# A decoder step's sample tokens: retention state on VectorE with transposed states, and each stream's second head pair bound to its own first

## The chip, the cores and the metric

The kernel runs on one core of a Trainium2 chip. The metric is device time in microseconds of one execution, the median of several runs. The profile shows one further execution, instruction by instruction. TensorE (PE) multiplies matrices into PSUM, VectorE (DVE) and ScalarE (ACT) do element work, SyncE (SP) issues nearly all DMAs from one in-order queue, and GpSimd (POOL) does almost nothing here.

## The reference

Two layers of a decoder trunk, for a prompt of 512 tokens and for 8 sample tokens (one new token of each of 8 sequences, each with its own state). Every layer is half an FFN, a token mixer, half an FFN, each with a layer norm. The mixer of layer 0 has four retention heads beside an RG-LRU; that of layer 1 is a pooling mixer. The part that matters is the retention step:

```python
q = rotary(q, pos) * (RET_DK ** -0.5); k = rotary(k, pos)
...
def step(s, qkv):          # one chunk; for a sample token the chunk has length 1
    scores = einsum('bhid,bhjd->bhij', qc, kc) * decay
    o = einsum('bhij,bhjv->bhiv', scores, vc) + einsum('bhid,bhdv->bhiv', qc * q_dec, s)
    s = s * c_dec + einsum('bhjd,bhjv->bhdv', kc * k_dec, vc)
    return s, o
...
mu = mean(o, -1); var = mean(square(o - mu), -1)
o = (o - mu) * rsqrt(var + LN_EPS) * gn_g
ret_out = silu(g) * o
```

For a sample token and a head with decay gamma this is: new state S' = gamma S + k v^T (128x128 for each of the 8 sequences), output o = S'^T q. The new states are outputs of the kernel too.

## The kernel before, in words

The 520 tokens are two streams that share the weights: stream A (s = 0) holds prompt tokens 0 to 255, stream B (s = 1) prompt tokens 256 to 511 and the 8 sample tokens, so matmuls of A have 256 columns and those of B 264. Features lie on partitions. A weight block arrives by DMA as raw fp32 (`load`, L422) in one of 36 SBUF slots, ACT rounds it to `hi` and DVE computes `lo` = raw - hi (`prep`, L434), and a *unit* (`emit`, L540) is 24 matmuls (hi x hi, hi x lo, lo x hi for eight 128-blocks) into one of five PSUM buffers `ps`, which ACT or DVE then evacuates. Everything else uses three more PSUM buffers `pm`.

The mixer of layer 0 has for each stream 4 units `ux`, then per head 4 units (q, k, v, g), with 4 units `ug` between heads 1 and 2 (`MIX_ORDER`), then 8 output units (`mk_mixout`). Around the units run generator tasks: `lru_task`, `ret_task` (retention of one head and stream) and `ret_finish` (group norm and gate of a pair of heads, 0 and 1 or 2 and 3). A small planner (`run`, L508) steps units and tasks in a virtual time and so sets the order in which instructions are emitted, in which slots are claimed (`get`, `slot`, `drop`) and weights prefetched (`wcap`, `dma_ahead`). Each task carries a priority offset (`D_RET = -200`, ...). The Tile layer then places the instructions on the engines by readiness and priority, so that the order on an engine can differ from that of emission; each engine runs its own list in order.

The sample tokens of a head are handled by `sample_ret` (L1187), called at the end of `ret_task` of stream B (L1139):

- the old states are loaded as S0[k, b, v], k on partitions, 512 bytes a run (L1193);
- k and v of the 8 tokens are transposed on PE (L1196, L1197); ACT copies k, DVE writes v times an 8x8 mask into an 8x1024 block VB (L1201);
- two matmuls with 8 rows and 512 columns form k v^T for four sequences each (L1209), and DVE adds gamma S0 (L1212, 128x512 twice);
- the new state is stored (L1215), and for each token one matmul of one column with S0 as the stationary operand gives o (L1220); ACT copies it, a matmul with the matrix of 1/128 gives its mean (L1228), which DVE subtracts (L1230).

Only then does `ret_task` set `retdone` and go on into `ret_finish`. In the unit list, the q unit of heads 2 and 3 waits for the flag `retdone1` of head h - 2 (L809), and `ret_finish` sets it for **both** streams at its end in stream B (L1183 to L1185): 

```python
dep=[("retdone1", h - 2)] if j == 0 and h >= 2 else []      # L809
...
            if s == 1:                                       # L1183
                self.flags[("retdone1", h, 0)] = 0.0
                self.flags[("retdone1", h, 1)] = 0.0
```

Of the kernel before, what the change touches and what calls it, by code (L numbers as in the profile page):

```python
# [58 lines left out]
D_LRU = 0  # L59
D_RET = -200  # L60
D_LN = 0
D_POOL = 0
D_PREP = 100
D_PREPP = 500
# [31 lines left out]
class Build:  # L96
    def __init__(self, ctx, tc, ins, outs):
        self.tc, self.nc = tc, tc.nc
        self.ins, self.outs = ins, outs
        self.t_pe = self.t_dve = self.t_act = self.t_pool = 0.0  # L100
        self.cpool = ctx.enter_context(tc.tile_pool(name="cp", bufs=1))
        self.spool = ctx.enter_context(tc.tile_pool(name="sp", bufs=NSLOT))
        self.tpool = ctx.enter_context(tc.tile_pool(name="tp", bufs=2))
        self.pp = ctx.enter_context(tc.tile_pool(name="pp", bufs=5, space=bass.MemoryType.PSUM))
        self.pm = ctx.enter_context(tc.tile_pool(name="pm", bufs=3, space=bass.MemoryType.PSUM))
        self.free = NSLOT
        self.wused = 0
        self.pmfree = 3
        self.tasks = []
        self.uid = 0  # L110
        self.flags = {}
        self.ntask = 0
        self.pin = False
# [107 lines left out]
    def alloc(self):  # L221
# [17 lines left out]
        self.HTAIL = [self.const(f"htail{s}", [P, 4]) for s in range(2)]  # L239
        self.US = self.const("us", [P, 4, NS])  # L240
        self.HS = self.const("hs", [P, 4, NS])
        self.SMP = self.const("smp", [P, 4, HEADS, NS])
        self.sp4 = self.const("sp4", [P, 4])
        self.pbs = self.const("pbs", [P, NCH])
        self.pss = self.const("pss", [P, NCH])
# [774 lines left out]
    def mk_qkvg(self, h, j):  # L1020
        def evac(s, ps, T):
# [7 lines left out]
            if j < 2:  # L1029
                sw = self.tmp("e")  # L1030
                rt = self.tmp("e")
                self.act(Tm(T.t), sw[0:64, :n], ps[64:128, :n])
                self.act(T, sw[64:128, :n], ps[0:64, :n])
                o = OFF[s]
                self.tt(Tm(T.t), rt[:, :n], ps[:, :n], self.cos[:, o:o + n], ALU.mult)
                self.tt(T, sw[:, :n], sw[:, :n], self.sin[:, o:o + n], ALU.mult)
                self.tt(T, qk[:, j, :], rt[:, :HALF], sw[:, :HALF], ALU.add)
                if s == 1:
                    self.tt(T, self.SMP[:, j, h, :], rt[:, HALF:n], sw[:, HALF:n], ALU.add)
                    if j == 0:  # L1040
                        self.ts(T, self.SMP[:, j, h, :], self.SMP[:, j, h, :], QSCALE, ALU.mult)
            else:
                f = AF.Copy if j == 2 else AF.Silu
                self.act(T, qk[:, j, :], ps[:, :HALF], f)
                if s == 1:
                    self.act(T, self.SMP[:, j, h, :], ps[:, HALF:n], f)
            if j == 2:
                self.spawn(self.ret_task(h, s, T), d=D_RET)
            if j == 3:
                self.flags[("sg", h, s)] = T.t  # L1050
        return evac
# [6 lines left out]
    def ret_task(self, h, s, T):  # L1058
# [11 lines left out]
        if h % 2 == 0:  # L1070
            self.RP[s] = self.slot([P, 4, NN[1]])
        B = self.RP[s]
        scs = self.slot([P, 4, HALF])
        ob = B[:, h % 2, :n]
        kt = B[:, 2 + h % 2, :HALF].rearrange("p (c k) -> p c k", c=2)
# [55 lines left out]
        if s == 0:  # L1131
            self.SPART[h] = so
        else:
            pa = self.SPART.pop(h)
            self.tt(Ts, so[:], so[:], pa[:], ALU.add)
            self.ts(Ts, so[:, :P], so[:, :P], so[:, P:P + 1], ALU.add)
            nc.sync.dma_start(self.outs["retp"][h], so[:, :P])
            yield ("v", None)
            yield from self.sample_ret(h, ob, scs, T)  # L1139
        self.drop(1)  # L1140
        self.flags[("retdone", h, s)] = T.t
        if h % 2:
            yield from self.ret_finish(h // 2, s, T)

    def ret_finish(self, pr, s, T):
        n = NN[s]
        B = self.RP[s]
        yield from self.get(1)
        Q = self.slot([P, 4, NN[1]])
# [30 lines left out]
            self.drop(1 + pr)  # L1180
        for h in (2 * pr, 2 * pr + 1):
            self.flags[("ret", h, s)] = T.t
            if s == 1:  # L1183
                self.flags[("retdone1", h, 0)] = 0.0
                self.flags[("retdone1", h, 1)] = 0.0  # L1185

    def sample_ret(self, h, ob, scs, T):  # L1187
        nc = self.nc
        yield from self.get(1)
        S0 = self.slot([P, NS, P])  # L1190
        VB = scs.rearrange("p a b -> p (a b)").rearrange("p (b v) -> p b v", b=NS)
        T0 = Tm(self.t_pe + 5.0)
        nc.sync.dma_start(S0[:], self.ins["sret"][0, :, h, :, :].rearrange("b k v -> k b v"))  # L1193
        yield from self.pmget(1)
        pk = self.pmt()
        self.tr(pk[:NS, :P], self.SMP[:, 1, h, :])  # L1196
        self.tr(pk[:NS, P:2 * P], self.SMP[:, 2, h, :])  # L1197
        Tk = Tm(self.t_pe + .1)
        ks = self.tpool.tile([NS, P], F32, tag="ks", name=self.nm("ks"), bufs=2)
        self.act(Tk, ks[:], pk[:NS, :P])  # L1200
        self.tt(Tk, VB[:NS, :, :], pk[:NS, P:2 * P].rearrange("p (a v) -> p a v", a=1).to_broadcast([NS, NS, P]),  # L1201
                self.s("mask8")[:NS, :].rearrange("p (b a) -> p b a", a=1).to_broadcast([NS, NS, P]), ALU.mult)
        self.pmfree += 1
        Tk.t = max(Tk.t, T0.t)
        yield ("pe", Tk)
        for hf in range(2):
            yield from self.pmget(1)
            po = self.pmt()
            self.mm(po[:], ks[:], VB[:NS, 4 * hf:4 * hf + 4, :].rearrange("p b v -> p (b v)"), True, True)  # L1209
            T.t = max(T.t, self.t_pe + 0.1)  # L1210
            sv = S0[:, 4 * hf:4 * hf + 4, :].rearrange("p b v -> p (b v)")
            self.stt(T, sv, sv, GAMMA[h], po[:], ALU.mult, ALU.add)  # L1212
            self.pmfree += 1
            yield ("v", None)
        nc.sync.dma_start(self.outs["rets"][:, h, :, :].rearrange("b k v -> k b v"), S0[:])  # L1215
        yield from self.pmget(1)
        yield ("pe", T)
        pq = self.pmt()
        for b in range(NS):
            self.mm(pq[:, b:b + 1], S0[:, b, :], self.SMP[:, 0, h, b:b + 1], True, True)  # L1220
        T.t = self.t_pe + .1
        self.drop(1)
        self.act(T, ob[:, HALF:NN[1]], pq[:, :NS])
        self.pmfree += 1
        yield from self.pmget(1)
        yield ("pe", T)
        pq = self.pmt()
        self.mm(pq[:, :NS], self.s("ones"), ob[:, HALF:NN[1]], True, True)  # L1228
        T.t = self.t_pe + .1
        self.tt(T, ob[:, HALF:NN[1]], ob[:, HALF:NN[1]], pq[:, :NS], ALU.subtract)  # L1230
        self.pmfree += 1


    def pool_task(self, s, T):
# [56 lines left out]

_OUT_SHAPES = dict(
    y=(P, NCH, NTOK), retp=(HEADS, P, P), hp=(P, 4), convp=(P, 4, 3), poolp=(P, NCH, PB),
    rets=(NS, HEADS, P, P), hs=(P, 4, NS), convs=(P, 4, 3, NS), pools=(P, NCH, NS, PB))


def _tables():
# [26 lines left out]
def _pack(i):  # L1324
# [36 lines left out]
    def put(n, a):  # L1361
# [23 lines left out]
    lruw = np.concatenate([i["lru_wa"][0], i["lru_wi"][0]], 0).transpose(1, 0, 2)  # L1385
    spool = i["state_pool"][0].reshape(NS, PB, NCH, P).transpose(3, 2, 0, 1)
    return dict(xa=xT[:, :, :HALF], xb=xT[:, :, HALF:], w8=np.stack(w8), w7=np.stack(w7), small=sm, lruw=lruw,
                rot=np.stack([cos, sin], 1), dec=dec, sret=i["state_ret"], spool=spool)


# [30 lines left out]
```

## Time and profile before

| | |
|---|---|
| median of 3 runs | 1837.92 us (1837.45 to 1840.04) |
| the profiled execution | 1838.75 us |
| its span, first to last instruction | 1836.8 us |
| PE / ACT / DVE / POOL busy | 98% / 38% / 49% / 0% of the span |
| mean granted TensorE clock | 0.99 of full speed |
| mixer of layer 0, roughly | 395 to 650 us of the span |

Read it from the top: PE is busy almost throughout, so a microsecond of PE work is a microsecond of time wherever PE does not wait. "Idle before" and a name in brackets say what an instruction of that engine waited for. The granted clock is 1.00 when the throttle lets TensorE run at its upper level (2.4 GHz) and 0.50 at the lower (1.2 GHz).

### The profile page before, as it was taken

The numbers are of one execution on the slowest core, as the hardware profiler recorded it, in microseconds if no ns is written. First come the engines' busy times: TensorE is split into PE (matmuls) and PEld (weight loads), VectorE is DVE, ScalarE is ACT, GpSimd is POOL, SyncE is SP. The second block draws the span as 40 slices with busy tenths as digits, with TensorE's granted clock in tenths as the row PEclk, the third lists the DMA queues.
The fourth block names the chain that finished last, engine by engine and source line by source line (L and its number), as shares of the span: only waits on it lengthen the run. The fifth ranks groups of instructions, "written<-read, shape, count | busy, mean of one in ns | idle before, by whom it ended". The sixth has DMA issues, their size and how long they took to land.

```text
span 1836.8 us, 33833 instructions
## 1 busy us (share of the span) xinstructions
PE 1798.1 (98%) x14727; PEld 1773.8 (97%) x14727; DVE 909.1 (49%) x1629; ACT 691.4 (38%) x1210; POOL 2.1 (0%) x10
## 2 busy tenths in 40 slices
PE   8999999999899999999999999999999899999997
PEld 8999999999889999999999999999999799999997
DVE  5443343497665884333335833333347843333336
ACT  5322222266654573222223732222225742222223
POOL 0000000000000000000000000000000000000000
PEclk9999999999989999999999999999999999999998
DMA  7323232223042422322322323223259822323311
GB/s 262 93 84 96 87 102 84 73 88 104 1 162 96 140 77 88 90 93 91 102 83 91 106 82 101 91 85 104 74 81 98 71 89 96 93 87 98 97 31 47
DMA packets 77380, 170.74 MB, mean 93 GB/s; under 512 B 24368, under 2 KB 37168, under 8 KB 77232
## 3 DMA queue, kind: packets, MB, share of 16 engines
q1 hardware_dynamic: 77232, 168.58, 32.5%
q8 instruction: 115, 1.88, 0.4%
q14 instruction: 33, 0.27, 0.0%
HBM read 163.44 MB, written 5.12 MB: 92 GB/s over the span
## 4 chain that ended last, share of the span: by engine, by line
PE 86%; DVE 7%; ACT 5%; issue 1%; DMA 0%; SPq 0%; ACTq 0%; DVEq 0%
PE ps L207 83%; PE pm L207 3%; ACT sl L185 3%; DVE sl L190 2%; DVE sl L203 2%; DVE x L190 1%; ACT L692 1%; ACT L185 1%; ACT xh L185 1%; DVE xl L190 0%; DMA x<-in_xa 0%; DVE x L203 0%; ACT x L185 0%; ACT e L185 0%; DVE e L190 0%
## 5 line engine op out<-in xcount | busy, mean ns | idle before, releaser
L207 PE MATMUL ps<-xh,sl 128*128 128x264 f32 (+1 forms) x6400 | 1172.3, 283 | 12.6 <-ACT xh L185 7.0
L207 PEld LDWEIGHTS ps<-xh,sl 128*128 128x128 f32 x6400 | 997.5, 189 | 16.4 <-ACT xh L185 8.1
L207 PE MATMUL ps<-xl,sl 128*128 128x264 f32 (+1 forms) x3200 | 902.9, 283 | 4.1 <-DVE xl L190 3.8
L207 PEld LDWEIGHTS ps<-xl,sl 128*128 128x128 f32 x3200 | 606.6, 190 | 6.5 <-DVE xl L190 5.9
L207 PE MATMUL ps<-sl,sl 128*128 128x264 f32 (+1 forms) x4672 | 586.7, 284 | 4.3 <-DVE sl L203 4.0
L207 PEld LDWEIGHTS ps<-sl,sl 128*128 128x128 f32 x4672 | 569.1, 189 | 8.9 <-DVE sl L203 5.3
L185 ACT ACTIVATE sl<-sl 128x1024 fp32r<-128x1024 f32 (+8 forms) x371 | 348.9, 950 | 461.2 <-PE ps L207 417.1
L190 DVE TENSOR_TENSOR sl<-sl,sl 128x1024 fp32r<-128x1024 f32 (+3 forms) x320 | 373.7, 1174 | 246.3 <-ACT sl L185 226.2
L190 DVE TENSOR_TENSOR e<-sil,ps 128x256 f32<-128x256 f32 (+1 forms) x176 | 74.7, 424 | 300.5 <-PE ps L207 298.5
L203 DVE SCALAR_TENSOR_TENSOR x<-ps,x 128x256 f32<-128x256 f32 (+1 forms) x208 | 88.5, 426 | 240.5 <-PE ps L207 240.4
L185 ACT ACTIVATE sl<-e 128x264 fp32r<-128x264 f32 (+1 forms) x184 | 76.5, 416 | 278.8 <-DVE e L190 277.8
L185 ACT ACTIVATE sil<-ps 128x264 f32<-128x264 f32 (+1 forms) x176 | 67.0, 382 | 188.4 <-PE ps L207 187.4
L190 DVE TENSOR_TENSOR sl<-e,sl 128x264 fp32r<-128x264 f32 (+1 forms) x184 | 78.5, 427 | 61.2 <-ACT sl L185 61.1
L190 DVE TENSOR_TENSOR x<-x,sl 128x512 f32<-128x512 f32 (+2 forms) x136 | 87.1, 677 | 2.8 <-ACT sl L185 1.8
L185 ACT ACTIVATE e<-x 128x256 f32<-128x256 f32 (+1 forms) x87 | 35.2, 416 | 54.2 <-DVE x L203 54.1
L185 ACT ACTIVATE xh<-x,small 128x256 fp32r<-128x256 f32 (+1 forms) x64 | 35.0, 596 | 9.1 <-DVE x L190 9.1
L185 ACT ACTIVATE sl<-pm 128x256 f32<-128x256 f32 (+2 forms) x44 | 15.0, 362 | 49.0 <-PE pm L207 49.0
L190 DVE TENSOR_TENSOR xl<-x,xh 128x512 fp32r<-128x512 f32 (+1 forms) x40 | 27.6, 695 | 6.3 <-ACT xh L185 5.8
L190 DVE TENSOR_TENSOR sl<-sl,e 128x256 f32<-128x256 f32 (+1 forms) x63 | 26.8, 425 | 1.4 <-ACT e L185 0.2
L185 ACT ACTIVATE x<-x,small 128x256 f32<-128x256 f32 (+1 forms) x44 | 25.7, 596 | 4.5 <-DVE x L190 4.3
L185 ACT ACTIVATE e<-ps 64x256 f32<-64x256 f32 (+3 forms) x40 | 15.3, 382 | 24.0 <-PE ps L207 18.4
L203 DVE SCALAR_TENSOR_TENSOR sl<-sl,sl 128x1024 f32<-128x1024 f32 (+3 forms) x14 | 15.0, 1084 | 18.1 <-ACT sl L185 18.0
(115 smaller groups left out, 480.9 us busy)
## 6 DMA issues: line engine op xcount, KB each, us to landing
sl<-in_w SPq DMA_DIRECT2D x241, 512.0 KB, 3.7
sl<-in_w SPq DMA_DIRECT2D x64, 448.0 KB, 3.3
sl<-in_sret SPq DMA_DIRECT2D x4, 512.0 KB, 5.7
out_rets<-sl SPq DMA_DIRECT2D x4, 512.0 KB, 3.6
x<-in_xb SPq DMA_DIRECT2D x2, 528.0 KB, 9.7
out_y<-x SPq DMA_DIRECT2D x4, 264.0 KB, 2.3
x<-in_xa SPq DMA_DIRECT2D x4, 256.0 KB, 6.7
sl<-in_dec SPq DMA_DIRECT2D x2, 512.0 KB, 4.5
```

The lines of the kernel that those rows point to most:

```text
L185: r = self.nc.scalar.activation(out, in_, func, scale=scale, **kw)
L190: r = self.nc.vector.tensor_tensor(out=out, in0=a, in1=b, op=op)
L203: self.nc.vector.scalar_tensor_tensor(out=out, in0=a, scalar=s, in1=b, op0=op0, op1=op1)
L207: self.nc.tensor.matmul(out, lhsT, rhs, start=start, stop=stop)
L692: self.nc.scalar.preload_act_table_set(LNEXP)
```

## The change

The states of the sample tokens are handed over and back by the host as [head][v][b][k] in place of [b][head][k][v], so the tile S0 has v on partitions and, along a partition, 8 tokens by 128 k, in one run of 4 KB.

As soon as k of a head (stream B) is rotated, its 8 q rows and 8 k rows are written transposed to a DRAM tile `KQ` (16 rows of 128, source 128 partitions of 16 elements). A new task `sample_task`, spawned at the v unit of stream B, takes two slots, reads the 8 k rows back broadcast to all 128 partitions (512 KB) and the states (512 KB), multiplies k by v (128x1024, v broadcast along k), adds gamma S0 (128x1024), stores the state, reads the q rows broadcast into the same tile, multiplies by the state and sums over k (128x1024 to 128x8). The mean over v is taken by the matmul with 1/128 as before, and the subtraction writes into the pair's output tile. The two transposes, the two 512-column matmuls and the eight one-column matmuls of each head, the mask product and the two ACT copies are gone.

`ret_finish` becomes a task of its own; for stream B it waits for the two heads' `sdone` flags. `retdone1` is set for the stream that has finished, so heads 2 and 3 of a stream follow that stream's own first pair.

```diff
-        self.SMP = self.const("smp", [P, 4, HEADS, NS])
+        self.SMPH = self.const("smp", [P, HEADS, 4, NS])
+        self.SMP = self.SMPH.rearrange("p h j b -> p j h b")
...
                     if j == 0:
                         self.ts(T, self.SMP[:, j, h, :], self.SMP[:, j, h, :], QSCALE, ALU.mult)
+                    else:
+                        self.KQ[h] = self.dpool.tile([2 * NS, P], F32, tag="kq", name=self.nm("kq"))
+                        self.nc.sync.dma_start(self.KQ[h][:].rearrange("a k -> k a"),
+                                               self.SMPH[:, h, 0:2, :].rearrange("p j b -> p (j b)"))
...
             if j == 2:
                 self.spawn(self.ret_task(h, s, T), d=D_RET)
+                if s == 1:
+                    self.spawn(self.sample_task(h, Tm(T.t)), d=D_SMP)
...
-            yield from self.sample_ret(h, ob, scs, T)
         self.drop(1)
         self.flags[("retdone", h, s)] = T.t
         if h % 2:
-            yield from self.ret_finish(h // 2, s, T)
+            self.spawn(self.ret_finish(h // 2, s, T), d=D_FIN if h == 1 else D_RET)
 
     def ret_finish(self, pr, s, T):
         n = NN[s]
+        while s == 1 and any(("sdone", 2 * pr + e) not in self.flags for e in range(2)):
+            yield ("w", None)
...
-            if s == 1:
-                self.flags[("retdone1", h, 0)] = 0.0
-                self.flags[("retdone1", h, 1)] = 0.0
+            self.flags[("retdone1", h, s)] = 0.0
...
+    def kqb(self, h, j):
+        t = self.KQ[h][j * NS:(j + 1) * NS, :]
+        return t.rearrange("(o b) k -> o b k", o=1).to_broadcast([P, NS, P])
+
+    def sample_task(self, h, T):
+        v = self.SMP[:, 2, h, :].rearrange("p (b a) -> p b a", a=1).to_broadcast([P, NS, P])
+        yield from self.get(2)
+        S0, KB = self.slot([P, NS, P]), self.slot([P, NS, P])
+        self.nc.sync.dma_start(KB[:], self.kqb(h, 1))
+        self.nc.sync.dma_start(S0[:], self.ins["sret"][h])
+        T.t = max(T.t, self.t_pe + SMP_DMA)
+        yield ("v", None)
+        self.tt(T, KB[:], KB[:], v, ALU.mult)
+        yield ("v", None)
+        self.stt(T, S0[:], S0[:], GAMMA[h], KB[:], ALU.mult, ALU.add)
+        self.nc.sync.dma_start(self.outs["rets"][h], S0[:])
+        self.nc.sync.dma_start(KB[:], self.kqb(h, 0))
+        T.t += SMP_DMA
+        yield ("v", None)
+        self.tt(T, KB[:], KB[:], S0[:], ALU.mult)
+        o = self.tpool.tile([P, NS], F32, tag="so8", name=self.nm("so8"), bufs=2)
+        yield ("v", None)
+        self.nc.vector.tensor_reduce(out=o[:], in_=KB[:], axis=AX.X, op=ALU.add)
+        self._adv("t_dve", 1.1, T)
+        self.drop(2)
+        while ("rb", h) not in self.flags:
+            yield ("w", None)
         yield from self.pmget(1)
         yield ("pe", T)
         pq = self.pmt()
-        for b in range(NS):
-            self.mm(pq[:, b:b + 1], S0[:, b, :], self.SMP[:, 0, h, b:b + 1], True, True)
+        self.mm(pq[:, :NS], self.s("ones"), o[:], True, True)
         T.t = self.t_pe + .1
-        self.drop(1)
-        self.act(T, ob[:, HALF:NN[1]], pq[:, :NS])
+        self.tt(T, self.RP[1][:, h % 2, HALF:NN[1]], o[:], pq[:, :NS], ALU.subtract)
...
-                rot=np.stack([cos, sin], 1), dec=dec, sret=i["state_ret"], spool=spool)
+                rot=np.stack([cos, sin], 1), dec=dec, sret=i["state_ret"][0].transpose(1, 3, 0, 2), spool=spool)
```

New constants: `D_SMP = 100`, `D_FIN = 0`, `SMP_DMA = 4.0`. The DRAM pool for `KQ` has two buffers.

## Rows read from the trace of the kernel before

**Rows 1.** The page, part 1: busy us (share of the span) and instructions of each engine.

```profile
PE 1798.1 (98%) x14727; PEld 1773.8 (97%) x14727; DVE 909.1 (49%) x1629; ACT 691.4 (38%) x1210; POOL 2.1 (0%) x10
```

**Rows 2.** Stretches: length, busy us (instructions) per engine, granted clock, DMA share, GB/s.

```profile
482.70:489.50 6.80, 5.34 (x25) 5.34 (x26) 6.55 (x8) 2.25 (x5) 0.00 (x0) 0.50 0.00 0
533.90:540.70 6.80, 6.80 (x29) 6.39 (x29) 1.45 (x4) 3.11 (x7) 0.00 (x0) 0.50 0.98 337
609.00:615.80 6.80, 6.80 (x33) 6.80 (x33) 2.47 (x7) 1.13 (x3) 0.00 (x0) 0.50 0.86 296
440.00:640.00 200.00, 190.13 (x1388) 178.82 (x1388) 141.43 (x315) 104.06 (x208) 0.21 (x1) 0.94 0.31 102
```

**Rows 3.** Timeline of PE around head 0's sample work: start, us, instruction, count.

```profile
502.57 0.38 PE L212 MATMUL pm<-small,smp 128*8 128x128 f32 x2
502.70 0.37 PE L207 MATMUL ps<-xh,sl 128*128 128x264 f32 x1
...
511.39 1.98 PE L207 MATMUL pm<-sl,ks 8*128 8x512 f32 x4
513.30 0.39 PE L207 MATMUL ps<-xh,sl 128*128 128x256 f32 x1
...
514.24 0.95 PE L207 MATMUL pm<-smp,sl 128*128 128x1 f32 x8
515.05 0.37 PE L207 MATMUL ps<-xl,sl 128*128 128x256 f32 x1
```

**Rows 4.** Timeline of PE, head 1's one-column matmuls.

```profile
531.61 1.05 PE L207 MATMUL pm<-smp,sl 128*128 128x1 f32 x8
...
533.44 1.28 PE L207 MATMUL pm<-smp,sl 128*128 128x1 f32 x8
```

**Rows 5.** DVE groups by shape: line, operation, out<-in, count | busy us, mean ns | idle before.

```profile
L203 DVE SCALAR_TENSOR_TENSOR sl<-sl,sl 128x1024 f32<-128x1024 f32 x5 | 6.0, 1225 | 6.8 <-ACT sl L185 6.8
L203 DVE SCALAR_TENSOR_TENSOR sl<-sl,pm 128x512 f32<-128x512 f32 x8 | 5.5, 687 | 2.3 <-PE pm L207 2.3
L190 DVE TENSOR_TENSOR sl<-pm,small 8x1024 f32<-8x1024 f32 x4 | 4.8, 1210 | 0.0
...
L190 DVE TENSOR_TENSOR sl<-sl,sl 128x1024 f32<-128x1024 f32 x3 | 3.7, 1220 | 2.8 <-ACT sl L185 2.8
...
L1271 DVE TENSOR_REDUCE ss<-sl 128x16 f32<-128x240 f32 x1 | 0.4, 394 | 0.0
```

**Rows 6.** DMA issues: queue, operation, count, KB each, median us from issue to landing.

```profile
sl<-in_w SPq DMA_DIRECT2D x241, 512.0 KB, 3.7
sl<-in_sret SPq DMA_DIRECT2D x4, 512.0 KB, 5.7
...
out_retp<-so SPq DMA_DIRECT2D x4, 64.0 KB, 1.5
...
out_pools<-xsm SPq DMA_DIRECT2D x1, 32.0 KB, 21.3
```

**Rows 7.** Waits of SP's queue: line waited for, us in total, times, longest.

```profile
SPq L1137 <- DVE sl L190: 53.2, 1, 53.2
```

**Rows 8.** Timeline of PE: three waits in brackets, second pair's start, stream B's first finish.

```profile
481.74 0.39 PE L207 MATMUL ps<-xh,sl 128*128 128x256 f32 x1 [3.36 <-ACT sl L185]
484.16 0.79 PE L207 MATMUL ps<-xh,sl 128*128 128x256 f32 x2 [1.92 <-DVE sl L190]
...
508.73 0.28 PE L207 MATMUL ps<-xl,sl 128*128 128x256 f32 x1
...
537.55 1.96 PE L207 MATMUL pm<-sl,small 128*128 128x264 f32 x4
...
625.67 0.51 PE L207 MATMUL ps<-sl,sl 128*128 128x264 f32 x2 [0.22 <-ACT sl L185]
```

**Rows 9.** Timeline of DVE: head 3's rotated sample k, and its sample output less the mean.

```profile
584.05 0.16 DVE L190 TENSOR_TENSOR smp<-e,e 128x8 f32<-128x8 f32 x1
...
613.54 0.16 DVE L190 TENSOR_TENSOR sl<-sl,pm 128x8 f32<-128x8 f32 x1 [3.84 <-PE pm L207]
```

More of the change, by code (lines that the diff above doesn't have):

```diff
@@ L61 @@
 D_LN = 0
+D_SMP = 100
+D_FIN = 0
+SMP_DMA = 4.0
 D_POOL = 0
@@ L103, in __init__ @@
         self.tpool = ctx.enter_context(tc.tile_pool(name="tp", bufs=2))
+        self.dpool = ctx.enter_context(tc.tile_pool(name="dp", bufs=2, space=bass.MemoryType.DRAM))
+        self.KQ = {}
         self.pp = ctx.enter_context(tc.tile_pool(name="pp", bufs=5, space=bass.MemoryType.PSUM))
@@ L1072, in ret_task @@
         B = self.RP[s]
+        self.flags[("rb", h) if s else ("ra", h)] = 0.0
         scs = self.slot([P, 4, HALF])
@@ L1182, in ret_finish @@
             self.flags[("ret", h, s)] = T.t
-            if s == 1:
-                self.flags[("retdone1", h, 0)] = 0.0
-                self.flags[("retdone1", h, 1)] = 0.0
[L1187 to L1215, printed above, removed]
@@ L1218, in sample_ret @@
         pq = self.pmt()
-        for b in range(NS):
-            self.mm(pq[:, b:b + 1], S0[:, b, :], self.SMP[:, 0, h, b:b + 1], True, True)
+        self.mm(pq[:, :NS], self.s("ones"), o[:], True, True)
         T.t = self.t_pe + .1
-        self.drop(1)
-        self.act(T, ob[:, HALF:NN[1]], pq[:, :NS])
+        self.tt(T, self.RP[1][:, h % 2, HALF:NN[1]], o[:], pq[:, :NS], ALU.subtract)
         self.pmfree += 1
[L1225 to L1231, printed above, removed]
+        self.flags[("sdone", h)] = T.t
     def pool_task(self, s, T):
@@ L1293 @@
     y=(P, NCH, NTOK), retp=(HEADS, P, P), hp=(P, 4), convp=(P, 4, 3), poolp=(P, NCH, PB),
-    rets=(NS, HEADS, P, P), hs=(P, 4, NS), convs=(P, 4, 3, NS), pools=(P, NCH, NS, PB))
+    rets=(HEADS, P, NS, P), hs=(P, 4, NS), convs=(P, 4, 3, NS), pools=(P, NCH, NS, PB))
 def _tables():
@@ L1414 @@
         np.ascontiguousarray(o["poolp"].transpose(2, 1, 0)).reshape(1, 1, PB, DM),
-        o["rets"].reshape(1, NS, HEADS, P, P),
+        np.ascontiguousarray(o["rets"].transpose(2, 0, 3, 1)).reshape(1, NS, HEADS, P, P),
         np.ascontiguousarray(o["hs"].transpose(2, 1, 0)).reshape(1, NS, 512),
```

## The prediction, made before the change was run

> **What bounds the kernel now.** I read the page's busy shares first. PE is busy 1798.1 of 1836.8 us [rows 1], so PE work that disappears is time that disappears, as long as nothing else becomes late in its place. Then I cut the mixer of layer 0 into stretches. In 440 to 640 us, where everything that the change touches lies, PE is busy 190.1 of 200 us at a mean clock of 0.94, DVE 141.4 and ACT 104.1 [rows 2]. So the stretch has two kinds of loss beside PE's own work: some 10 us of idle PE, and time at the lower clock. Three of the half-clock stretches are 6.8 us long each [rows 2]. The timeline of PE tells what came ahead of each. Ahead of the first, PE idled 3.36 and 1.92 us waiting for the two halves of a weight block, from ACT and from DVE [rows 8]. Ahead of the second stand the sample matmuls of head 1: the first eight one-column records cover 531.61 to 532.66 and the second eight begin at 533.44, just where the clock falls [rows 2, 4]. The third, 609.0 to 615.8, begins in the same work of head 3. That a run of such thin matmuls is what lets the clock fall is an inference: heads 0 and 2 have the same matmuls, more thinly mixed with units, and no such stretch.
>
> **What the change removes from PE.** Head 0 runs at full clock and gives the prices. I take the distance from the start of a piece to the start of the next unit matmul, since PE overlaps instructions. The transposes of k and v take 0.13 us (502.57 to 502.70), the two 512-column matmuls 1.91 (511.39 to 513.30), one half of the one-column matmuls 0.81 (514.24 to 515.05), and so both 1.62 [rows 3]. That is 3.66 us a head, **14.6 us** for four. All of it lies among unit matmuls on a busy PE, so it counts in full. The mean matmul with 1/128 stays.
>
> **What it gives back of the clock.** If PE has only unit matmuls around heads 1 and 3, the two stretches of 6.8 us go, and each had done half of what it could: 3.4 us each, **6.8 us** together [rows 2]. The bounds are 0 (the clock falls anyway) and 6.8; I take 6.8, because the thin matmuls stand right ahead of both.
>
> **What it adds on DVE and takes from DVE and ACT.** Per head two products of 128x1024 at 1.22, one fused multiply-add at 1.225, and one sum over 1024 elements. The nearest row for the sum has 240 elements and 394 ns, by which 1024 would take 1.7 us; as low a price as a plain product, 1.22, bounds it below. I take 1.4, so 5.1 us a head. Gone are two of 0.687 and one of 1.21: 2.6 us [rows 5]. Net 2.5 us a head, 10 us in all, on an engine with 58 us free in this stretch [rows 2]. I cost it at nothing; what hides it is PE's backlog in five PSUM buffers. If DVE were the late engine throughout, it would cost those 10 us. ACT loses two small copies a head, which is worth nothing off the path.
>
> **What it adds in DMA and on SP's queue.** Per head: a write of 8 KB in 2048 runs of 4 bytes, two broadcast reads of 512 KB, the state read and the state write, the last two now in runs of 4 KB. Five issues replace two. The trace has one write with 4-byte runs, 8192 of them, that landed in 21.3 us [rows 6]. A quarter of it gives 5.3 us, and if the count did not matter it would be 21.3; a write of 64 KB in long runs, 1.5 us, is the floor [rows 6]. I take 5.3, as the runs are of the same kind. A broadcast read is in no row. Its bounds are the weight block's 3.7 and the old state read's 5.7 for the same bytes [rows 6], and I take 4.7; 128 reads of the same 4 KB could also be slower than either, and that stays in the range. SP is in order: the k read waits there for the write to land, the state write for DVE's multiply-add, the q read for that too, and the weight loads stand behind them. What that costs is bounded by what SP already bears: a store of head 0's prompt state held the queue for 53.2 us [rows 7], and the waits that PE shows in those 53 us name ACT and DVE halves and no DMA. Waits of 5 to 10 us should cost nothing, so I take 0; if the prefetch ran dry, a hole like that at 481 us would follow (below).
>
> **The new order of the streams.** The flag of the second pair holds back emission, not visibly PE: A's second pair starts at 508.73, 29 us ahead of B's first finish at 537.55 that sets the flag, with unit matmuls on PE up to it [rows 8]. So the edit has no wait of its own to remove. It can still move the hole at 478 to 490 us: if A's q unit of head 2 has its weight halves ready there, PE gains 3.36 + 1.92 = 5.3 idle and, of the half-clock stretch with 5.34 us of work in it, 2.7 more, 8.0 together [rows 2, 8]. If A's lead holds slots and weights longer, one more such hole opens, and it costs 8.0. Two extra slots per head in flight push in the same direction. I take 0, with both ends for the range.
>
> **The end of the mixer.** B's first output unit starts at 625.67 after a wait of only 0.22 [rows 8]: there PE's own work and B's chain (sample output at 613.54, group norm, gate) come out even, so I check both. PE gets there 14.6 + 6.8 = 21.4 us earlier, at about 604.0. Head 3's k is ready at 584.05 [rows 9], and this moves up by three heads' matmuls and one clock stretch, 14.4 us. From k to the sample output I count write 5.3, read 4.7, product and multiply-add 2.4, read 4.7, product and sum 2.6: 19.7 us, to 603.8 in place of 613.54 [rows 9], 9.7 earlier. B's chain is then ready at 625.67 - 14.4 - 9.7 = 601.6, with 2.4 us to spare. With slower reads (5.7 each) and a write of 8 it is 2.3 late, and retention of the prompt tokens may then be last. I take **2 us back**, with 0 and 5 as ends.
>
> **Sum.** 14.6 + 6.8 - 2 = 19.4 us. The profiled execution took 1838.75, 0.83 above the median of the runs shown, 1837.92. So 1837.92 - 19.4 = **1818.5**. Not counted is the slower start of the first unit matmul behind each removed piece, which could add a microsecond. The case itself spans 1811 to 1828.
>
> **Rivals.**
> First, *DVE is held by loads* (slower). The multiplies by k and by q wait for a read from DRAM, eight times. DVE is in order, so a multiply placed too early holds the evacuations of PSUM behind it (rotary products, FFN products, `lo` halves), and PE stops once its five buffers are full. It decides against the change from 19.4 / 8 = 2.4 us of lost PE per wait. If a multiply is placed right behind its issue, DVE waits the whole 3.7 to 5.7; with 4 us lost each, 32 us are lost and the time is about 1850. For it: DVE is the busiest engine after PE here. Against: no DVE row of this stretch waits for a DMA, the old state read included, and some of each wait is covered by PSUM. Chance 0.20, of which 0.03 for mild waits that end near no change.
>
> Second, *the transposing write is the late one*. From a landing of 5.3 + 2.4 = 7.7 us on, B's output units wait for it. At 21.3 the sample output comes 16 us later than counted, B's chain is ready at 617.6, PE idles 13.6 and then runs 3.4 at the lower clock: 1837.92 - 21.4 + 17.0 = 1833.5, within a hair of no change. Chance 0.07.
> The Trainium skill speaks against the change at this place: its page "DMA: Bandwidth & Descriptors", section "Rules for kernel authors", says that a transpose should not be made by a plain DMA with a rearranged access pattern and gives a factor of 19. Applied to the 1.5 us write this is an estimate of 28.5 us and a time of about 1841. By that rule the trace half agrees: 32 KB in 4-byte runs took 21.3 us where 64 KB took 1.5 [rows 6], but the run count here is a quarter.
>
> Third, *the hole at 478 us is filled* by A's second pair: 1818.5 - 8.0 = 1810.5. For it: PE has nothing to do there but wait for weights. Against: it is ACT and DVE that are late there, and they are no earlier. Chance 0.14.
>
> Fourth, *the clock falls anyway*, at a new place or the same: only the matmuls' 14.6 less 2 stay, 1825.3. Chance 0.13. The forecast has 0.46.
>
> **How the numbers follow.** What a measurement of this kernel can tell from no change is about 0.2%, 3.7 us. Faster: 0.46 + 0.14 + 0.13 = 0.73. Within: 0.07 + 0.03 = 0.10. Slower: the rest of the first rival, 0.17. The range runs from 1806 (the filled hole with the uncounted microseconds) to 1840 (the late write and mild DVE waits) and leaves out the bulk of the first rival.
>
> **What would show it.** In the new profile the one-column and 8-row matmuls are absent, and PE has 3.7 us less per head. The stretches around heads 1 and 3 stay at 1.00. No DVE instruction names a DMA as releaser, and PE's waits name no multiply of the sample task. The write lands in about 5 us, the broadcast reads in 4 to 6. B's first output unit starts near 604 with a wait under 5. The forecast is wrong if PE's idle time in the mixer grows by more than 15 us, whatever ends it.

## The result, and the profile after

The changed kernel takes 1861.07 us (median of four runs, 1857.56 to 1864.56) against 1838.2: ratio 1.0126, 95% interval 1.0114 to 1.0139. It is 22.9 us slower where 19.4 us faster was forecast, and above the top of the forecast range, 1840. The profiled execution took 1863.19 us, 24.4 above the one of before (1838.75).

The page's first part for the changed kernel answers [rows 1]: PE is busy 8.1 us less, and the span is 24.3 us longer, so PE waits.

```profile
span 1861.1 us, 33673 instructions
PE 1790.0 (96%) x14639; PEld 1768.3 (95%) x14639; DVE 918.0 (49%) x1633; ACT 690.2 (37%) x1202; POOL 2.1 (0%) x10
```

The mixer of layer 0 up to the same unit (the first of the FFN behind it, 647.8 before, 668.3 after) shows where. Columns as in [rows 2]. Before:

```profile
396.00:648.00 252.00, 241.84 (x1807) 229.47 (x1806) 182.61 (x393) 144.50 (x283) 0.98 (x4) 0.95 0.29 95
```

After, and below it the stretch that answers the last of [rows 2]:

```profile
396.00:668.30 272.30, 231.03 (x1705) 221.53 (x1705) 192.01 (x400) 143.88 (x276) 0.99 (x4) 0.91 0.39 103
440.00:640.00 200.00, 159.02 (x1137) 150.67 (x1136) 131.43 (x285) 92.02 (x180) 0.21 (x1) 0.89 0.45 115
```

The mixer is 20.3 us longer. PE works 10.8 us less in it, although more of the work is at the lower clock (mean 0.91 for 0.95), and idles 41.3 us for 10.2: 31.1 more. The remaining 4 of the 24.3 us lie behind the mixer; I found no cause for them, and executions of this kernel spread over 7 us.

PE's timeline in the mixer of the changed kernel, the waits above 3 us (in brackets the idle time and what ended it):

```profile
458.66 0.39 PE L212 MATMUL ps<-xh,sl 128*128 128x256 f32 x1 [3.80 <-ACT sl L190]
...
488.63 0.58 PE L212 MATMUL ps<-xh,sl 128*128 128x256 f32 x1 [4.62 <-ACT sl L190]
...
568.34 0.58 PE L212 MATMUL ps<-xh,sl 128*128 128x256 f32 x1 [5.38 <-ACT sl L190]
...
607.74 1.22 PE L212 MATMUL pm<-sl,so 128*128 128x256 f32 x2 [9.57 <-DVE sl L195]
...
621.36 0.57 PE L212 MATMUL pm<-so,small 128*128 128x8 f32 x2 [3.76 <-DVE so L1221]
...
639.00 8.86 PE L212 MATMUL ps<-sl,sl 128*128 128x256 f32 x53 [3.81 <-DVE x L208]
```

Before, only the hole at 478 to 490 us was of this size [rows 8]. Two kinds are new. At 458.66 and 568.34 a unit waits for ACT's half of a weight block. From 607.74 on, PE waits for stages of the retention, and at 639.00 for DVE to evacuate an output unit (`x` <- `ps`). The chain of waits says what is behind each (start, us, what):

```profile
444.03 13.50 DMA sl<-in_w
...
553.93 13.28 DMA sl<-in_w
...
589.62 12.26 DMA kq<-smp
601.94 4.17 DMA sl<-kq
```

A weight block that landed in 3.7 us [rows 6] takes over 13 here, twice, and late in the mixer the transposing write takes 12.26 and the broadcast read behind it 4.2. The DMA view gives the landings (count, size, median us):

```profile
sl<-kq SPq DMA_DIRECT2D x8, 512.0 KB, 5.5
...
kq<-smp SPq DMA_DIRECT2D x4, 8.0 KB, 12.2
```

SP's timeline shows why the weights are late: they are issued right behind the write, in the same queue.

```profile
443.56 0.38 SPq L1050 DMA_DIRECT2D kq<-smp  x1
444.03 1.31 SPq L432 DMA_DIRECT2D sl<-in_w  x2
455.56 0.33 SPq L1207 DMA_DIRECT2D sl<-kq  x1
```

ACT's and DVE's timelines show the two engines waiting for these transfers: first ACT for the weights issued at 444.03, then DVE's multiply by the k rows of head 3.

```profile
457.56 1.06 ACT L190 ACTIVATE sl<-sl 128x1024 fp32r<-128x1024 f32 x1 [7.31 <-DMA sl<-in_w]
```

```profile
606.13 1.23 DVE L195 TENSOR_TENSOR sl<-sl,smp 128x1024 f32<-128x1024 f32 x1 [10.15 <-DMA sl<-kq]
```

DVE works its list in order, so this multiply holds up everything behind it. PE's wait of 9.57 us ends at 607.74, 1.6 us after the multiply has started.

### The profile page after: what moved, and what is told of

It reads as the page before. It is cut to its first block, busy times and chain, and to the rows that moved or that the text cites. A ratio compares the mean times of both kernels' runs of the same rounds, so it can differ in the third digit from the quotient of the medians.

```text
span 1861.1 us, 33673 instructions
## 1 busy us (share of the span) xinstructions
PE 1790.0 (96%) x14639; PEld 1768.3 (95%) x14639; DVE 918.0 (49%) x1633; ACT 690.2 (37%) x1202; POOL 2.1 (0%) x10
## 4 chain that ended last, share of the span: by engine, by line
PE 83%; DVE 7%; ACT 6%; DMA 3%; issue 1%; SPq 0%; ACTq 0%; DVEq 0%
PE ps L212 81%; ACT sl L190 3%; DVE sl L195 2%; PE pm L212 2%; DVE sl L208 2%; DMA sl<-in_w 1%; DVE x L195 1%; ACT L698 1%; ACT L190 1%; DMA kq<-smp 1%; ACT xh L190 1%; DMA sl<-kq 1%; DVE xl L195 0%; ACT x L190 0%; DMA x<-in_xa 0%
## 5 line engine op out<-in xcount | busy, mean ns | idle before, releaser
L212 PE MATMUL ps<-xh,sl 128*128 128x264 f32 (+1 forms) x6400 | 1169.0, 283 | 23.3 <-ACT sl L190 13.8
L212 PEld LDWEIGHTS ps<-xh,sl 128*128 128x128 f32 x6400 | 996.3, 189 | 27.1 <-ACT sl L190 14.6
L195 DVE TENSOR_TENSOR sl<-sl,sl 128x1024 fp32r<-128x1024 f32 (+4 forms) x324 | 378.7, 1174 | 258.6 <-ACT sl L190 236.7
L190 ACT ACTIVATE e<-x 128x264 f32<-128x264 f32 (+1 forms) x87 | 34.9, 416 | 56.7 <-DVE x L208 56.5
L190 ACT ACTIVATE sl<-pm 128x256 f32<-128x256 f32 (+1 forms) x40 | 14.4, 382 | 56.6 <-PE pm L212 56.6
L208 DVE SCALAR_TENSOR_TENSOR sl<-sl,sl 128x1024 f32<-128x1024 f32 (+3 forms) x18 | 19.9, 1113 | 21.3 <-ACT sl L190 21.2
```

Of the source, the lines that this page charges most:

```text
L190: r = self.nc.scalar.activation(out, in_, func, scale=scale, **kw)
L195: r = self.nc.vector.tensor_tensor(out=out, in0=a, in1=b, op=op)
L208: self.nc.vector.scalar_tensor_tensor(out=out, in0=a, scalar=s, in1=b, op0=op0, op1=op1)
L212: self.nc.tensor.matmul(out, lhsT, rhs, start=start, stop=stop)
```

## The experiments

**Theory after the result:** the write with 4-byte runs costs twice, once because loads issued behind it on SP's queue arrive no sooner than it does, and once because the sample chain gets its k late. **Rivals:** the broadcast reads and the multiplies on DVE are the cost (the first rival of the prediction); the new order of the streams is; SP's waits are, and not the landing; the removal never was worth what I counted.

### The same kernel with long runs in the write

```diff
-self.nc.sync.dma_start(self.KQ[h][:].rearrange("a k -> k a"),
+self.nc.sync.dma_start(self.KQ[h][:].rearrange("a k -> (a k)").rearrange("(p f) -> p f", p=P),
```

> The changed kernel with one difference: the 16 rows of key and query are written to DRAM untransposed, 128 runs of 64 bytes in place of 2048 runs of 4 bytes, so the broadcast rows hold the right numbers in the wrong places and the sample tokens' retention is wrong; the instructions of TensorE, VectorE and ScalarE and their order are the same as in the changed kernel. Theory W (the transposing write is what costs: it lands in 12.2 us, holds the weight loads issued behind it and makes the sample multiplies late): the write lands in about 2 us, the weight loads behind it in 4 in place of 13, PE's waits of 4.6, 5.4, 9.6 and 3.8 us go with their half-clock stretches, and the time falls from 1861 to 1818 to 1830. Rival O (the second pairs' new order costs the time): no change of order here, so 1855 to 1863. Rival L (the broadcast reads and VectorE's waits for them cost it, however the write is laid out): 1848 to 1858.

Measured: 1831.69 us, ratio 0.9963 (0.9950 to 0.9976). That is 1.7 us above the range of theory W and far below those of the rivals. The 8 KB land in 1.4 us, the broadcast reads in 5.1, and PE's order is that of the changed kernel but for a handful of instructions. So the form of this one write is worth 29.4 us, and reads, multiplies, order and SP's wait for k are all still in a kernel that is 6 us faster than before. That wait can be named: the write waits 61.7 us in all for DVE's k here, 62.2 in the changed kernel, and in both two weight loads stand behind the first write (issued at 443.51 here). SP's other new wait, that of the k read for the write to land, did shrink, from 30.4 to 1.3 us; the run on ACT's queue below has it at its longest. Here those two land in 4.1 us and no unit waits at 458. What is left of long PE waits in this kernel:

```profile
480.88 0.58 PE L212 MATMUL ps<-xh,sl 128*128 128x256 f32 x1 [4.82 <-ACT sl L190]
...
593.98 0.56 PE L212 MATMUL pm<-so,small 128*128 128x8 f32 x2 [4.02 <-DVE so L1221]
611.63 4.61 PE L212 MATMUL ps<-sl,sl 128*128 128x256 f32 x20 [3.85 <-DVE x L208]
```

The first is the old hole of [rows 8]. The other two are the end of the mixer, which comes back below.

### The writes alone, in the kernel before

The four transposing writes are added to the kernel before, where they stand in the changed one, with the sample tile laid out by heads as there. Nobody reads them.

```diff
...
 self.ts(T, self.SMP[:, j, h, :], self.SMP[:, j, h, :], QSCALE, ALU.mult)
+else:
+    self.KQ[h] = self.dpool.tile([2 * NS, P], F32, tag="kq", name=self.nm("kq"))
+    self.nc.sync.dma_start(self.KQ[h][:].rearrange("a k -> k a"),
+                           self.SMPH[:, h, 0:2, :].rearrange("p j b -> p (j b)"))
```

> The kernel before with the four transposing writes of key and query rows added (2048 runs of 4 bytes each), which nobody reads; the sample tokens' retention stays on TensorE. If the writes hurt by holding the weight loads issued behind them (theory W1), some loads take 13 us in place of 4 and the time is 1843 to 1856, with PE waits for weight halves. If they hurt only because the sample multiplies wait for them (theory W2), 1834 to 1841.

Measured: 1852.31 us, ratio 1.0083 (1.0068 to 1.0098), 14.5 us for 32 KB of output that nothing waits for. The chain of waits and PE's timeline of this kernel show the weights again:

```profile
444.24 13.24 DMA sl<-in_w
...
560.69 6.75 DMA sl<-in_w
```

```profile
458.62 0.38 PE L209 MATMUL ps<-xh,sl 128*128 128x256 f32 x1 [3.56 <-ACT sl L187]
...
554.25 1.12 PE L214 MATMUL pm<-small,sl 128*128 128x128 f32 x4 [4.12 <-ACT sl L187]
575.00 0.39 PE L209 MATMUL ps<-xh,sl 128*128 128x256 f32 x1 [2.57 <-ACT sl L187]
```

The first is where the changed kernel has its first new wait, 458.66. The one at 554.25 is for a stage of the retention and not for a weight half; the kernel before has it too, with 2.10 us at 547.07.

### The write issued from ACT's queue

```diff
-self.nc.sync.dma_start(self.KQ[h][:].rearrange("a k -> k a"),
+self.nc.scalar.dma_start(self.KQ[h][:].rearrange("a k -> k a"),
```

> The changed kernel with one difference: the transposing write is issued from ScalarE's queue, the weight loads stay on SyncE's. The first broadcast read still waits for the write. If the weight loads behind it are late because they stand behind it in the same queue's rings (theory W1a), they land in 4 to 6 us, PE's waits of 4.6 and 5.4 us for weights go, the 9.6 us for head 3's product stays, and the time is 1843 to 1852. If the 16 DMA engines themselves are full (theory W1b), loads still take 10 us and more and the time is 1855 to 1863.

Measured: 1847.56 us, ratio 1.0053 (1.0037 to 1.0070): 13.5 below the changed kernel, near the 14.5 of the run above. The write still lands in 11.1 us. No weight load stands on the chain any more, the PE waits at 458.66 and 568.34 are gone, and what is left is the late k:

```profile
574.63 11.44 DMA kq<-smp
586.12 4.16 DMA sl<-kq
```

```profile
591.91 1.22 PE L212 MATMUL pm<-sl,so 128*128 128x256 f32 x2 [8.67 <-DVE sl L195]
605.22 0.56 PE L212 MATMUL pm<-so,small 128*128 128x8 f32 x2 [4.23 <-DVE so L1221]
622.45 3.90 PE L212 MATMUL ps<-sl,sl 128*128 128x256 f32 x22 [3.77 <-DVE x L208]
```

SP's wait for the landing is no rival any more: the k reads hold SP for 69.0 us here, over twice the time in the changed kernel, and no unit waits for a weight beyond the old hole at 481 us. The changed kernel, then this one:

```profile
SPq L1207 <- DMA kq<-smp: 30.4, 3, 11.0
```

```profile
SPq L1207 <- DMA kq<-smp: 69.0, 3, 26.2
```

This run has a limit. SP no longer waits for k, so the loads that stood behind the first write are now issued 16 us ahead of it:

```profile
427.64 2.00 SPq L432 DMA_DIRECT2D sl<-in_w  x4
```

I found no weight load under way during a write here. So the run shows that loads kept from behind the write are not late, and not that a second queue would carry them past it. The Trainium skill, page "DMA: Bandwidth & Descriptors", section "Issuing engines are not separate DMA queues", says that transfers started by different engines share the same DMA engines and that starting them elsewhere saves only the time to issue. Nothing here speaks against that, but an edit of that kind still gave 13.5 us, by the order in which things were issued.

### The order of the streams, alone and taken away

First the kernel before with the new flag, then the changed kernel with the old one:

```diff
-if s == 1:
-    self.flags[("retdone1", h, 0)] = 0.0
-    self.flags[("retdone1", h, 1)] = 0.0
+self.flags[("retdone1", h, s)] = 0.0
```

> The kernel before with one difference: the flag that lets heads 2 and 3 start is set for the stream that has finished its first pair, not for both at the end of stream B's. The sample tokens' retention stays on TensorE. Theory W: about as before, 1830 to 1846. Rival O: slower by some 20 us, 1855 or more. Rival L: as W.

> The changed kernel with one difference: the flag for heads 2 and 3 is set for both streams at the end of stream B's first pair, as before. Theory W: the four transposing writes are still there, so 1855 to 1867. Rival O: 1838 or less. Rival L: 1855 to 1867.

Measured: 1837.35 us for the order alone, ratio 0.9999 (0.9989 to 1.0009), and 1859.97 for the rest without it, 1.0114 (1.0099 to 1.0129). By itself the order is worth nothing, and the loss is there without it.

### The removal alone, in both orders

The sample retention is left out of the changed kernel: the old state is loaded and stored as it is, and q + k stands for the output, so neither PE nor DVE does the sample work.

```diff
-self.nc.sync.dma_start(KB[:], self.kqb(h, 1))
...
-self.tt(T, KB[:], KB[:], v, ALU.mult)
-self.stt(T, S0[:], S0[:], GAMMA[h], KB[:], ALU.mult, ALU.add)
...
-self.nc.vector.tensor_reduce(out=o[:], in_=KB[:], axis=AX.X, op=ALU.add)
+self.tt(T, o[:], self.SMP[:, 0, h, :], self.SMP[:, 1, h, :], ALU.add)
```

> The changed kernel with the sample tokens' retention taken off TensorE and nothing put in its place: the old state is loaded and stored as it is, the output of a token is the sum of its key and query, and no transposing write, broadcast read, product or sum over k is left. It shows what the removal alone is worth in the new order. If the terms of the prediction hold (14.6 us of PE and 6.8 us of clock, 2 given back; theory P), 1815 to 1822. If the norms at the end of the mixer and new half-clock stretches take part of it back whatever the sample tokens do (theory N), 1824 to 1832.

> The run with the sample tokens' retention left out (old state stored as it is, output of a token the sum of its key and query), with one more difference: heads 2 and 3 of both streams start when stream B's first pair is done, as before. If the new order of the second pairs is worth nothing by itself (theory Z), 1825 to 1831, within 3 us of the 1828 with the new order. If it is what hinders PE from using the 16 us that the removal frees (theory O2), 1815 to 1822.

Measured: 1827.94 us with the new order, 0.9947 (0.9932 to 0.9962), and 1823.3 with the old, 0.9921 (0.9903 to 0.9938). The first lies in the range of theory N, the second between those of Z and O2. So 9.9 and 15.1 us are what the change could bring if the sample work on DVE were free, and the last rival is right in part: with the new order the removal is worth only half of what I counted. With the old order the mean clock of 440 to 640 us rises to 0.97 (0.94 before), with the new one it stays at 0.94: there new waits for weight halves open on PE, with half-clock stretches at them, the longest 4.65 us at 538.10 (the old order has one of 3.30 at 523.22). At the end of the mixer the new order has no PE wait above 1 us, so it is not the norms there that take the gain back. The old order has one, without any sample work:

```profile
602.83 8.09 PE L213 MATMUL ps<-sl,sl 128*128 128x256 f32 x53 [4.03 <-DVE x L209]
```

### k and q transposed on PE

If long runs are the cure, one may make them: PE transposes the 128x16 tile into 16x128, ACT copies it out of PSUM, and 16 runs of 512 bytes go to DRAM.

```diff
-self.nc.sync.dma_start(self.KQ[h][:].rearrange("a k -> k a"),
-                       self.SMPH[:, h, 0:2, :].rearrange("p j b -> p (j b)"))
+self.spawn(self.kq_task(h, Tm(T.t)), d=D_KQ)      # D_KQ = 0
...
+def kq_task(self, h, T):
+    ...
+    self.tr(pk[:2 * NS, :P], self.SMPH[:, h, 0:2, :].rearrange("p j b -> p (j b)"))
+    self.act(Tk, ks[:], pk[:2 * NS, :P])
+    self.nc.sync.dma_start(self.KQ[h][:], ks[:])
```

> The changed kernel with one difference: key and query of the 8 tokens are transposed by one TensorE instruction per head into 16 rows, copied by ScalarE, and written to DRAM in 16 runs of 512 bytes. All results are computed. Theory W: the write lands in 2 us, the transposes cost some 0.2 us of PE a head, and the time is 1819 to 1832, below the kernel before. Rival O: 1855 to 1865. Rival L: 1848 to 1860.

Measured: 1832.77 us, ratio 0.9974 (0.9964 to 0.9984). It is the whole computation, and beats both kernels. The write lands in 1.3 us, the reads in 4.5. Of the 19.4 us, 4.9 are there; the time is 0.8 us above the range of theory W. The longest PE wait left in the mixer:

```profile
594.49 0.57 PE L213 MATMUL pm<-so,small 128*128 128x8 f32 x2 [6.49 <-DVE so L1235]
```

It waits for the sum over k of head 3 (`so`). Is it the sample chain that is late, or would another stage be late there anyway? Three runs on that:

### The q rows in a slot of their own, the sample work last, and the old order

The q rows are read right behind the k rows into a third slot, so the sum no longer waits for a read issued after the first product:

```diff
-S0, KB = self.slot([P, NS, P]), self.slot([P, NS, P])
+S0, KB, QB = self.slot([P, NS, P]), self.slot([P, NS, P]), self.slot([P, NS, P])
...
+self.nc.sync.dma_start(QB[:], self.kqb(h, 0))
```

> The kernel with TensorE transposes of key and query, with one more difference: the query rows are read into a tile of their own right behind the key rows, so that the read no longer waits for the multiply-add. All results are computed. If head 3's sample chain is what holds PE at the end of the mixer (theory S), PE's wait of 6.5 us for the sum goes and the time is 1824 to 1829. If stream A's group norm is due there anyway (theory N), 1830 to 1835.

Measured: 1832.57 us, 0.9975 (0.9964 to 0.9985), no change from the run above. The wait has only another name; now it is an output unit of stream A that waits for the gated retention:

```profile
598.05 0.80 PE L213 MATMUL ps<-sl,sl 128*128 128x256 f32 x2 [6.94 <-ACT sl L191]
```

So another stage is due there at the same time, as theory N said. Then the sample work is put behind everything else in the planner's order, on the thought that it takes DVE from stream A's group norm:

```diff
-D_SMP = 100
+D_SMP = 600
```

> The kernel with TensorE transposes and a tile of its own for the query rows, with one more difference: the sample task's priority offset is 600 in place of 100, so its VectorE work gives way to stream A's second group norm. All results are computed. If the two 128x1024 operations among that norm's VectorE work are what makes it late at the end of the mixer (theory D), PE's wait of 6.9 us there shrinks to under 4 and the time is 1826 to 1831. If the norm's own length is what PE meets once the cover is gone (theory N), 1830 to 1836.

Measured: 1855.11 us, 1.0101 (1.0084 to 1.0118). That thought was wrong, and the time is outside both ranges. PE's list is in order and holds the sample's own matmul with 1/128; made late, it stops PE (536.70, for the sum over k). Near the end PE waits for prompt retention on DVE (607.10) and for the gated retention (619.34), which is late all the same:

```profile
536.70 0.60 PE L213 MATMUL pm<-so,small 128*128 128x8 f32 x2 [5.59 <-DVE so L1234]
...
607.10 1.22 PE L213 MATMUL pm<-sl,so 128*128 128x256 f32 x2 [5.56 <-DVE sl L196]
...
619.34 0.80 PE L213 MATMUL ps<-sl,sl 128*128 128x256 f32 x2 [7.29 <-ACT sl L191]
```

Last, the PE transposes with the old order of streams:

> The kernel with TensorE transposes of key and query, with heads 2 and 3 of both streams started when stream B's first pair is done, as before. All results are computed. Theory Z: 1829 to 1837, as with the new order (1832.8). Theory O2: 1822 to 1827.

Measured: 1835.93 us, 0.9992 (0.9980 to 1.0003), 3.2 above the new order. This lies in the range of theory Z, which expected no difference. One wait grows in another place, where the changed kernel with the old order has 7.98 us too (548.55):

```profile
540.41 1.12 PE L218 MATMUL pm<-small,sl 128*128 128x128 f32 x4 [7.98 <-ACT sl L191]
```

The order is thus worth 0 alone, 4.6 against with the removal, 3.2 for with the PE transposes. It changes which weight halves or gates are due when PE comes, and no single price fits it.

### What makes the write slow

The writes nobody reads again, one form per head: 2048 runs of 4 bytes as in the change, 1024, 2048 with every element alone in 64 bytes of DRAM (`kw`), and 512.

```diff
+if h == 0:   self.nc.sync.dma_start(self.KQ[h][:].rearrange("a k -> k a"), src)
+elif h == 1: self.nc.sync.dma_start(self.KQ[h][0:NS, :].rearrange("a k -> k a"), src[:, 0:NS])
+elif h == 2: self.nc.sync.dma_start(wide[:, :, 0], src)          # wide: [P, 2 * NS, 16]
+else:        self.nc.sync.dma_start(self.KQ[h][0:4, :].rearrange("a k -> k a"), src[:, 0:4])
```

> The kernel before with one DRAM write per head that nobody reads, in four forms of 4-byte runs: head 0 the write of the change (2048 runs, neighbours in DRAM written by different partitions), head 1 half as many (1024), head 2 again 2048 runs with each element alone in 64 bytes, head 3 a quarter (512). If each run has its price (theory R), they land in about 12, 6.5, 12 and 4 us. If it is neighbouring elements that collide (theory N4), head 2's lands in under 7. If most of it is a fixed price of such a write (theory F), heads 1 and 3 stay above 9.

Measured: the four landings, in the order of the heads, each a single one; and 1857.34 us for the kernel, 1.0105 (1.0085 to 1.0125).

```profile
kq<-smp SPq DMA_DIRECT2D x1, 8.0 KB, 11.3
kq<-smp SPq DMA_DIRECT2D x1, 4.0 KB, 9.4
kw<-smp SPq DMA_DIRECT2D x1, 8.0 KB, 6.5
kq<-smp SPq DMA_DIRECT2D x1, 2.0 KB, 9.4
```

The time hardly follows the count of runs: a quarter of them takes 9.4 us in place of 11.3 (the four equal writes of the kernel with the writes alone landed in 11.6 to 11.8). It does depend on where they go: the same 2048 runs take 6.5 when no two of them share 64 bytes. Theories N4 and F both hold, R does not. In the change, 16 neighbouring elements come from 16 partitions. That this sharing is the cause is the reading nearest to the four numbers; the spread-out form also differs in its strides, which were not varied by themselves.

The harm to the loads behind a write does not shrink with the count of its runs either. This kernel is slower than the one with four full writes (1852.31). Its chain of waits has weight loads behind the first, the spread-out and the smallest write, and behind the smallest, 2 KB, PE has its longest wait, with no multiply by k on DVE at all:

```profile
445.38 12.92 DMA sl<-in_w
...
559.35 7.65 DMA sl<-in_w
...
589.61 12.73 DMA sl<-in_w
```

```profile
605.21 2.47 PE L209 MATMUL pm<-sl,sl 128*128 128x256 f32 x8 [9.69 <-DVE sl L192]
```

DVE's instructions ahead of 605.21 waited for ACT's half of that weight block. So loads behind a write can hold up the retention at the end of the mixer as well, in the way that the late k does in the changed kernel.

## Why the prediction was wrong, point by point

The runs put the 22.9 us together in steps, by their medians (before: 1837.7 to 1838.2 beside these runs, so the steps add up to 23.3):

| kernel | us | step |
|---|---|---|
| removal alone, new order | 1827.94 | -9.9 |
| with the sample work on DVE and the broadcast reads (long runs in the write) | 1831.69 | +3.8 |
| with the slow write, but no loads behind it (ACT's queue) | 1847.56 | +15.9 |
| with the loads behind it (the change) | 1861.07 | +13.5 |

Each step also shifts the order of the work a little, and the order of the streams alone moved two of these kernels by 3.2 and 4.6 us; I take the steps to be right to that, an estimate. The 14.5 us of the writes alone are a second measurement of the last.

**PE's removed work: right.** 14.6 us were counted. In the removal alone with the old order PE is busy 21.2 us less than the 1798.1 of [rows 1]:

```profile
PE 1776.9 (98%) x14639; PEld 1758.2 (97%) x14639; DVE 900.9 (49%) x1621; ACT 688.2 (38%) x1201; POOL 3.4 (0%) x10
```

Of these 5.1 are clock (by the clock records of the traces, half-clock time in 400 to 660 us is 23.9 us before and 13.7 there; half of the difference), and 16.1 the removed work. PE's waits in the mixer grow by 6.0 us in all (10.1 before), the 4.03 at its end among them: 21.2 - 6.0 = 15.2, and the run gained 15.1.

**The clock: right only there.** 6.8 were counted because the thin matmuls of heads 1 and 3 stand ahead of two half-clock stretches [rows 2, 4]. In the old order both go, but half as long ones open at the waits at 523.22 and 602.83, and 5.1 are left. In the changed kernel a half-clock stretch begins during or just behind each of the six PE waits above 3 us. The total stays at 23.9 us with the removal alone in the new order and with long runs, and doubles to 47.8 in the change. The fourth rival, "the clock falls anyway, at a new place", was right in this part. I had asked what let the clock fall before and not what new idle time would do, although [rows 2, 8] show exactly that at 482.7.

**DVE's work and the reads: right.** The DVE rows of the changed kernel in 440 to 640 us confirm the prices, the sum over k included (1.4 was taken):

```profile
L208 DVE SCALAR_TENSOR_TENSOR sl<-sl,sl 128x1024 f32<-128x1024 f32 x4 | 4.9, 1217 | 0.0
L1221 DVE TENSOR_REDUCE so<-sl 128x8 f32<-128x1024 f32 x4 | 4.9, 1215 | 0.0
```

The reads land in 5.5 us where 4.7 was taken between 3.7 and 5.7. With 6.3 in the run with the q rows in a slot of their own, the bound of 5.7 was too low. Both together cost about the 3.8 us of the second line of the table.

**The write: mis-sized.** This is the first step that failed: "A quarter of it gives 5.3 us ... as the runs are of the same kind." The bounds of 1.5 and 21.3 held the measured 12.2. The runs are not of the same kind. The row's write (`out_pools`, L1252) puts its elements 60 bytes apart; the nearest of the four forms, each element alone in 64 bytes, landed in 6.5, not far from 5.3. The change's write puts 16 partitions' elements side by side, and for that form a quarter of the runs still takes 9.4 us of 11.3, so there is hardly a price per run to scale by. The Trainium skill's rule that I quoted (page "DMA: Bandwidth & Descriptors", section "Rules for kernel authors") gave an estimate of 28.5 us. Against the 1.4 us of the same 8 KB in long runs, 12.2 is a factor of 8.7; the page's 19 is against a hardware transpose, which no run here has. Its warning was right all the same.

**The loads behind the write: the step that did most harm.** "The weight loads stand behind them ... so I take 0." I had priced the *wait* of the queue [rows 7], and there I was right: the run with long runs has the same 62 us of SP waiting for k, at no visible cost. I had not asked what a transfer does to the *next transfer* in its queue once it is issued. That is 13.5 to 14.5 us where I took 0, and no rival held it. The sentence after it, "if the prefetch ran dry, a hole like that at 481 us would follow", describes what came, twice.

**The late k: right mechanism, too cheap.** The second rival let the write be late from a landing of 7.7 us on, and moved only the end of the sample chain. At 12.2 its sum gives an end 4.5 us late. The step from 1.4 to 11.1 us of landing cost 15.9. What was left out is the first rival's mechanism, at one place: the multiply by the k rows of head 3 waits 10.15 us at the head of DVE's list, and the retention of prompt tokens behind it stops PE for 9.57. The first rival blamed the reads for this; without the slow write the four such multiplies show no wait and the four by the q rows 1.1 us in all.

**The order of the streams: right as 0**, with ends that were needed (-4.6 to +3.2 in company).

**The end of the mixer: too small.** 2 us back were counted, from the sample chain alone. With long runs the waits there are 4.02 and 3.85 us, the PE transposes have 6.49 and the q rows in a slot of their own 6.94, and with no sample work at all the old order has 4.03. A PE that comes earlier finds the sum over k, the gated retention of stream A, or DVE's evacuation of an output unit not ready; which one differs from run to run. With the new order and no sample work there is no such wait, so the group norm by itself does not explain them: in the new order they come with the sample work on DVE, and how much of them is that work and how much the order stays open. I had checked stream B's output unit and not stream A's.

My own test was the right one: "wrong if PE's idle time in the mixer grows by more than 15 us"; it grew by 31.1.

## What to carry to other kernels

Before a small strided DMA goes into a queue that also carries a prefetch, price what it does to the transfers issued behind it, apart from what it makes the queue wait: here 8 KB held up two 512 KB loads at once. Lay data out for long runs before it reaches DRAM, even at the price of a PE transpose and a copy (1832.8 against 1861.1 us). And when work is taken from a busy engine, look up each stage that becomes due earlier, for every stream, as some of them set the new time.

## What was new of the hardware

The write is slow after its data has moved. The DMA view of the kernel with the write on ACT's queue, 484.0 to 495.5 us in 40 slices (busy tenths of the DMA engines, then GB/s), has the second write alone, issued at 483.99 and landing 11.1 us later:

```profile
DMA  0005777400000000000000000000000000200010
GB/s 0 0 0 4 7 7 7 4 0 0 0 0 0 0 0 0 0 0 0 0 0 0 0 0 0 0 0 0 0 0 0 0 0 0 57 0 0 0 28 0
```

Its packets move within 1.5 us, and then nothing of it is seen for the 8 to 9 us up to its landing (the two late spots, 57 and 28 GB/s, are one packet each of the instruction queues q8 and q14). In the changed kernel, 443.5 to 457.0 us, two weight loads stand behind such a write:

```profile
DMA  0007775000090039949936899681965323115789
GB/s 0 0 0 6 7 7 5 0 0 0 0 97 0 0 12 73 133 12 36 24 24 24 36 49 36 12 36 12 36 24 12 12 24 24 12 24 146 243 364 401
```

They start, trickle at some 12 to 50 GB/s in most slices with the DMA engines shown busy, and 240 to 400 are reached only from about 456 us on, when the write has landed (443.56 + 11.9); the k read issued at 455.56 has a part in these. In the trace's packet records, 42 of the 78 packets of 4 KB that start in 444 to 456 us take over 1 us each, the longest 5.6, where the median of such a packet before the change is 0.16. What holds them no row shows. A broadcast read of 512 KB from 4 KB of DRAM landed in 4.5 us (with the PE transposes) to 6.3 (with the q rows in a slot of their own), where a weight block takes 3.7.
